# Neighbouring array groups for the state space products, and norms summed as their tiles are made

## The chip, the cores and the metric

One core of a Trainium2 chip runs the whole program. Its engines are TensorE (matrix products), VectorE, ScalarE, GpSimd and SyncE (which issues loads); they run side by side and wait for each other by semaphores. The metric is the device time of one execution in microseconds, the median of several.

## What is computed

The input is x of 512 tokens and 1024 features, a context of 256 tokens and a condition vector c. Two blocks follow each other. The first has a modulated norm, a two-way linear recurrence (LRU) beside a chunk-wise mixer, a second modulated norm with a convolutional feed-forward part, and a final norm:

```
rms(x, g)  = x * rsqrt(mean(x*x) + eps) * g
mod(x, g, shift, scale) = rms(x, g) * (1 + scale) + shift
m = silu(c) @ w_mod + b_mod                       # six rows: shift, scale, gate, twice
x = x + m[2] * mixer(mod(x, g1, m[0], m[1]) @ w_in)
x = x + m[5] * conv_ffn(mod(x, g2, m[3], m[4]))
h = rms(x, g_final)
```

The second block norms h again (mix_g) and adds two branches: S5, a complex diagonal state space, and an attention of 8 heads with a forget gate and with normed queries and keys. A third norm feeds a layer that picks 16 of 16384 experts per head and token:

```
xr, xi = u @ Br, u @ Bi                           # 32 groups of 16 inputs, 64 states
s_t    = lambda * s_(t-1) + x_t                   # complex
y      = sr @ Cr - si @ Ci + d * u
h = h + 0.25-scaled sum of glu(gelu(y)) and attention, through w_out
h = h + peer(rms(h, ffn_g))
```

## The kernel before

Everything lies with features on the 128 partitions and tokens along the row: a tensor of 1024 features is 8 tiles (k or d) of 128x512. The large products split both operands into a high and a low half (`split_w` L114 for weights: ScalarE copies the high half `whi`, VectorE subtracts for `wlo`; `split_to` L144 for activations) and need three products a tile (`mm3`, L121 to L123); `proj` makes one block of 128 output features from 8 tiles, 24 products.

A norm sums over features, so over partitions and tiles. `colsum` (L150) multiplies each squared tile by a block of ones, four tiles on the four groups of 32 output columns; `tok_mean` (L160) copies the result and turns the sums of 128 tokens into a column with a second small product, `c32` carrying the 1/1024; `rstd_of` (L166) takes root and reciprocal, and `bcast_tok` (L175, L176) spreads the result over all partitions as `pr` with four diagonal matrices `dg`. `scaled_split` (L181 to L186) multiplies a tile with `pr` and the gain, and splits it.

At the start SyncE loads the parameters, x, the context (`ct`) and the four modulation chunks of w_mod that this norm needs (chunks 0 and 1 are the shift's halves, 2 and 3 the scale's; two buffers `wm`). `mod_a` (L208) multiplies a chunk with the condition on four column groups, `mod_b` (L217 to L221) turns the result into columns of `modx` and `modc`. Then a loop over k (L278 on) scales, shifts and splits x and context tiles, and `lru_in` multiplies them with w_rx, two blocks a head.

The stages of the first block follow: LRU to 215 us, mixer with w_out to 637 us, the second norm with modulation chunks 10 and 11 (L208, ahead of it in the code), feed-forward to 1027 us, where `ffn_down` adds into x1, the final norm and the mixer norm one after the other to 1046 us. From 1060 to 1450 us an order written out by hand interleaves S5 and attention: for each pair of heads `a_proj`, `a_sums` (sums of squares of query and key, each on its own column group, L1032), `a_norm2` (spreads the reciprocal roots over partitions, L1044, and splits), `a_scores`, `a_trans`, `a_pv`, and between them 17 calls of `s5_step`. A step s of S5 stands for two groups, 32 inputs and 128 states: `s5_x` multiplies 32 rows of u with B's real and imaginary parts (L973, L974), VectorE rotates and scans them (L978 to L987), and in the next step `s5_y` (L1001) multiplies the four results with C into 32 partitions of `py`, four steps filling one `py`:

```
nc.tensor.matmul(pxr, BT[0][rows, q], uT[rows, q], start=True, stop=True)
nc.tensor.matmul(pxi, BT[1][rows, q], uT[rows, q], start=True, stop=True)
...
nc.tensor.matmul(py[32 * i:32 * i + 32], CD[c][:, s], x, start=n == 0, stop=n == 3)
...
nc.tensor.matmul(pb, selq[j], rs, start=True, stop=True)
```

Here `rows` are partitions 32i to 32i+32 with i = s mod 4, so neighbouring steps use neighbouring groups of 32 rows (B) and of 32 columns (C). w_glu and w2_out follow to 1567 us, then the third norm, transposes of x3, the queries, the selection (1582 to 1730 us) and the two expert stages with their gathers, which no part of the change touches. A scheduler orders each engine's instructions from the written order and the data, so a piece of code can move against its neighbours.

## Time and profile before

| what | value |
|---|---|
| time of three executions | 2935.10, 2935.18, 2942.08 us; median 2935.18 |
| profiled execution: time / span | 2937.33 / 2935.5 us |
| TensorE busy, products | 2846.1 us (97%) |
| TensorE's weight loads, beside them | 2293.1 us (78%) |
| VectorE, ScalarE, GpSimd busy | 1963.8, 1159.5, 404.2 us |
| mean granted clock of TensorE | 0.984 of full speed |
| instructions | 37882 |

PE is TensorE, PEld its weight loads, DVE VectorE, ACT ScalarE, POOL GpSimd, SP SyncE. A busy TensorE is not one at its peak: its products overlap in a pipeline, their ends are modelled, and a product alone is listed as longer than the distance to the next. A product in plain 32-bit is two records. The granted clock is a share of 2.4 GHz, so 0.5 is 1.2 GHz. An arrow names what ended an engine's wait. Idle time of an engine that nobody waits for costs nothing, so the shares are read stage by stage.

### The profile page before, as it was taken

To read this page: it belongs to the slowest core of one execution; us is meant where nothing else is said; L and a number is where in the kernel's file an instruction comes from. 1 tells how busy PE (TensorE), PEld (TensorE's weight loads), DVE (VectorE), ACT (ScalarE), POOL (GpSimd) and SP (SyncE) were. 2 spreads that over 40 slices of the span, in tenths; PEclk is the share of its full clock that TensorE was granted. 3 is DMA by queue.
4 is the path that set the end of the run, shared out by engine and by line. 5 is a ranking of instruction groups with operands and counts; after the bars stand their busy time and mean duration, and the time that the engine had idled before them with its cause. 6 is when DMAs were issued, how large, how long until landed. Compare 5 with 4: busy or idle time off the path is not lost.

```text
span 2935.5 us, 37882 instructions
## 1 busy us (share of the span) xinstructions
PE 2846.1 (97%) x14431; PEld 2293.1 (78%) x14431; DVE 1963.8 (67%) x3556; ACT 1159.5 (39%) x1599; POOL 404.2 (14%) x437
## 2 busy tenths in 40 slices
PE   8999999999999999999999989999989999999999
PEld 5778888867888866665787879898989977777776
DVE  6686894339767575777455999999875444444444
ACT  4666523223323333334433334555543333333332
POOL 0000000000000000000000034555433112222221
PEclk9999999999999999999999999999999999999999
DMA  6333363332333322222223258898997588888884
GB/s 253 111 128 96 102 195 118 102 124 93 98 96 93 103 103 72 74 72 63 94 93 115 84 172 309 301 330 315 329 353 269 195 294 295 309 304 318 315 309 161
DMA packets 167622, 540.16 MB, mean 184 GB/s; under 512 B 16912, under 2 KB 42128, under 8 KB 163984
## 3 DMA queue, kind: packets, MB, share of 16 engines
q1 hardware_dynamic: 128272, 391.94, 39.6%
q0 software_dynamic: 36864, 134.23, 12.4%
q10 hardware_dynamic: 2304, 11.57, 1.0%
q8 instruction: 113, 1.85, 0.3%
q14 instruction: 69, 0.57, 0.1%
HBM read 479.48 MB, written 58.20 MB: 183 GB/s over the span
## 4 chain that ended last, share of the span: by engine, by line
PE 80%; DVE 9%; issue 5%; ACT 2%; POOL 2%; DMA 1%; POOLq 0%; DVEq 0%; ACTq 0%
PE acc L1628 19%; PE pmm L121 15%; PE pmm L123 15%; PE pmm L122 15%; PE accg L1505 2%; PE pmm L1001 2%; DVE wlo L114 2%; POOL rows L1459 2%; DVE rows L1470 1%; PE pm L208 1%; PE pa L150 1%; PE pg L121 1%; PE pg L122 1%; PE pg L123 1%; PE pmm L973 1%
## 5 line engine op out<-in xcount | busy, mean ns | idle before, releaser
L113 ACT ACTIVATE whi<-raw 128x1024 fp32r<-128x1024 f32 (+2 forms) x502 | 518.1, 1033 | 910.6 <-PE pmm L122 741.7
L114 DVE TENSOR_TENSOR wlo<-raw,whi 128x1024 fp32r<-128x1024 f32 (+2 forms) x502 | 607.7, 1211 | 298.1 <-ACT whi L113 293.4
L123 PE MATMUL pmm<-nph,wlo 128*128 128x384 f32 (+1 forms) x1152 | 398.4, 346 | 18.5 <-DVE wlo L114 18.4
L121 PE MATMUL pmm<-nph,whi 128*128 128x384 f32 (+1 forms) x1152 | 405.1, 352 | 0.3 <-ACT whi L113 0.3
L122 PE MATMUL pmm<-npl,whi 128*128 128x384 f32 (+1 forms) x1152 | 396.5, 344 | 0.0
L144 DVE TENSOR_TENSOR wtl<-w,wth 128x384 fp32r<-128x384 f32 x128 | 71.3, 558 | 292.7 <-ACT wth L143 284.9
L1628 PE MATMUL acc<-whi,wth 128*128 128x512 f32 x768 | 245.0, 400 | 0.0
L1628 PE MATMUL acc<-wlo,wth 128*128 128x512 f32 x768 | 241.5, 396 | 0.0
L1628 PE MATMUL acc<-whi,wtl 128*128 128x512 f32 x768 | 241.5, 395 | 0.0
L123 PEld LDWEIGHTS pmm<-nph,wlo 128*128 128x128 f32 x1152 | 219.5, 191 | 27.9 <-DVE wlo L114 22.7
L121 PEld LDWEIGHTS pmm<-nph,whi 128*128 128x128 f32 x1152 | 220.2, 191 | 5.1 <-ACT whi L113 0.6
L122 PEld LDWEIGHTS pmm<-npl,whi 128*128 128x128 f32 x1152 | 220.0, 191 | 4.5
L143 ACT ACTIVATE wth<-w 128x384 fp32r<-128x384 f32 x128 | 67.1, 525 | 395.7 <-PE acc L1628 382.3
L1459 POOL DMA_INDIRECT rows<-in_peer_v_rows_dram,idxT x128 | 126.5, 988 | 503.5 <-PE accg L1505 400.5
L1470 DVE SCALAR_TENSOR_TENSOR rows<-rows,hN 128x1024 f32<-128x1024 f32 x128 | 155.0, 1217 | 50.3 <-DMA rows<-in_peer_u_rows_dram,idx 49.3
L1628 PEld LDWEIGHTS acc<-whi,wth 128*128 128x128 f32 x768 | 141.8, 188 | 58.6 <-ACT whi L113 26.8
L1459 POOL DMA_INDIRECT rows<-in_peer_u_rows_dram,idx x128 | 165.6, 1294 | 48.7 <-POOL rows L1458 26.4
L1628 PEld LDWEIGHTS acc<-wlo,wth 128*128 128x128 f32 x768 | 144.4, 188 | 34.9
L1628 PEld LDWEIGHTS acc<-whi,wtl 128*128 128x128 f32 x768 | 144.4, 188 | 34.8
L123 PE MATMUL pmm<-h2h,wlo 128*128 128x512 f32 x352 | 138.0, 394 | 2.8 <-DVE wlo L114 2.8
L121 PE MATMUL pmm<-h2h,whi 128*128 128x512 f32 x352 | 138.8, 396 | 1.7 <-ACT h2h L185 1.6
L122 PE MATMUL pmm<-h2l,whi 128*128 128x512 f32 x352 | 138.2, 394 | 0.1
(503 smaller groups left out, 5797.2 us busy)
## 6 DMA issues: line engine op xcount, KB each, us to landing
raw<-in_peer_u_dram SPq DMA_DIRECT2D x128, 512.0 KB
raw<-in_peer_v_rows_dram SPq DMA_DIRECT2D x128, 512.0 KB
GD<-G SPq DMA_DIRECT2D x12, 2048.0 KB
Gg<-GD SPq DMA_DIRECT2D x64, 384.0 KB
raw<-in_w_up_dram SPq DMA_DIRECT2D x44, 512.0 KB
AD<-act SPq DMA_DIRECT2D x48, 384.0 KB
act<-AD SPq DMA_DIRECT2D x48, 384.0 KB
raw<-in_w_mod_dram SPq DMA_DIRECT2D x32, 512.0 KB
```

What stands on the lines that cost most here:

```text
L113: nc.scalar.activation(hi[:, :n], raw[:, :n], AF.Copy)
L114: (eng or nc.vector).tensor_tensor(out=lo[:, :n], in0=raw[:, :n], in1=hi[:, :n].bitcast(F32), op=OP.subtract)
L121: nc.tensor.matmul(ps, wh, ah, start=first, stop=False)
L122: nc.tensor.matmul(ps, wh, al, start=False, stop=False)
L123: nc.tensor.matmul(ps, wl, ah, start=False, stop=last)
L143: nc.scalar.activation(hi, src, AF.Copy)
L144: nc.vector.tensor_tensor(out=lo, in0=src, in1=hi.bitcast(F32), op=OP.subtract)
L1001: nc.tensor.matmul(py[32 * i:32 * i + 32], CD[c][:, s], x, start=n == 0, stop=n == 3)
L1459: nc.gpsimd.indirect_dma_start(out=r, out_offset=None, in_=I[tab], in_offset=bass.IndirectOffsetOnAxis(ap=at, axis=0))
L1470: nc.vector.scalar_tensor_tensor(r, r, 1.0, hN, op0=OP.mult, op1=OP.mult, accum_out=dot[:, n:n + 1])
L1505: nc.tensor.matmul(acc[q][32 * g:32 * g + 32], w[:, g, 31 - c:63 - c], ready[g][:, q * 512:(q + 1) * 512], start=c == 0, stop=c == 31)
L1628: nc.tensor.matmul(acc[t][q], a[:, c], bb[:, q * 512:(q + 1) * 512], start=f, stop=l)
```

## The change

1. Start: loads come in the order chunk 2, chunk 0, two w_rx blocks, chunk 3, chunk 1. The squares of x are summed tile by tile on VectorE, those of the context on GpSimd, which also scales the context. The first half of the tiles is split after chunks 2 and 0, and the first two w_rx blocks are multiplied tile by tile as these come.
2. Norms: `SumSq` replaces `colsum` and `tok_mean`; each tile's square is added to one accumulator (GpSimd, or VectorE for the last), and one small product per 128 tokens gives the mean. It runs inside the loops of w_out, w_down and w2_out. After the second norm two w_up blocks advance tile by tile (`two`), and chunk 11 comes behind them. The final and the mixer norm take both sums at once and normalise by the product of their roots; two u blocks advance tile by tile. At the third norm one of four sets of transposes goes ahead.
3. S5 and attention: `s5_y` interleaves the products of step s with those of s-1; `s5_in` makes B's real part of the next step right behind the imaginary part of this one; `a_norm2` issues its four broadcasts together, each over its own 32 rows; three buffers for w1 and w2; one more call of `s5_step`.

The core of the diff:

```diff
+    class SumSq:
+        def add(self, src, eng=None, scale=1.0):
+            if self.k == 0:
+                nc.scalar.activation(self.acc, src, AF.Square, scale=scale)
+            else:
+                s = self.pool.tile([128, self.n], F32, name=self.sqtag, tag=self.sqtag, bufs=self.bufs)
+                nc.scalar.activation(s, src, AF.Square, scale=scale)
+                (eng or nc.vector).tensor_tensor(out=self.acc, in0=self.acc, in1=s, op=OP.add)
+            self.k += 1
+        def mean(self, pb):
+            for t in range(self.n // 128):
+                nc.tensor.matmul(pb[:, 2 * t:2 * t + 2], self.acc[:, t * 128:(t + 1) * 128], cD, start=True, stop=True)
+            return pb[:, 0:2 * (self.n // 128):2]
+    def sqrt_table():
+        nc.scalar.activation(junk, epsb, AF.Sqrt)
...
+    for ch in (2, 0, 3, 1):
+        wm[ch] = wk.tile([128, 8, 512], F32, name="wm", tag="wm", bufs=2)
...
+        if ch == 0:
+            rraw = [load_raw(I["w_rx"][n].rearrange("p k c -> p (k c)"), 1024) for n in range(2)]
...
+    for k in range(KT):
+        sc.add(ct[:, k], nc.gpsimd)
+    s_.append(mod_a(psp, wk, 0, whole=wm[0]))
+    rxw = [split_w(r, 1024) for r in rraw]
...
+    for k in range(KT):
+        nc.gpsimd.tensor_tensor(out=ct[:, k], in0=ct[:, k], in1=prcs, op=OP.mult)
...
+    h_tiles(0)
+    rx_mm(0, 2)
+    s_ = [mod_a(psp, wk, ch, whole=wm[ch], wide=ps2) for ch in (3, 1)]
+    rx_mm(2, 3)
+    for x, ch in zip(s_, (3, 1)):
+        mod_b(psp, x, ch, wide=ps2)
+    h_tiles(4)
+    rx_mm(3, KT)
...
         nc.vector.scalar_tensor_tensor(x1[:, d], pp, m2h[:, d:d + 1], x1[:, d], op0=OP.mult, op1=OP.add)
+        s2.add(x1[:, d], nc.gpsimd if d < KT - 1 else nc.vector)
...
+    r1 = rstd_of(const, s2.mean(psm()), T, "r1")
...
-    ms = [mod_a(ps, n2p, 10), mod_a(ps, n2p, 11)]
-    r1 = rstd_of(n2p, tok_mean(n2p, ps, sq_tiles(n2p, x1), T, "n2"), T, "r1")
-    mod_b(ps, ms[0], 10)
-    mod_b(ps, ms[1], 11)
+    ms = mod_a(ps, n2p, 10)
     pr = bcast_tok(n2p, ps, r1, T)
+    pg01 = [psm(), psm()]
     for k in range(KT):
         scaled_split(n2p, pr, A2[:, k:k + 1], x1[:, k], h2h[:, k], h2l[:, k], T, bias=modx[:, 24 + k:25 + k])
+        two(k, pg01, "w_up", (0, 1), h2h, h2l)
+    mod_b(ps, ms, 10)
+    mod_b(ps, mod_a(ps, n2p, 11), 11)
...
+        if k0 + kg == 22:
+            sa.add(x1[:, d], nc.gpsimd if d < KT - 1 else nc.vector)
+            sb.add(x1[:, d], scale=gf[:, d:d + 1])
...
+    for k in range(KT):
+        scaled_split(np_, pr12, gfm[:, k:k + 1], x1[:, k], hbh[:, k], hbl[:, k], T)
+        two(k, pu01, "w2_u", (0, 1), hbh, hbl)
...
+        px = S5["x", s, c] = psm()
+        nc.tensor.matmul(px, BT[c][rows, q], uT[rows, q], start=True, stop=True)
...
+        if s == 0:
+            s5_in(0, 0)
+        s5_in(s, 1)
+        if s < 15:
+            s5_in(s + 1, 0)
...
-        for n, (c, x) in enumerate(S5.pop(("s", s))):
-            nc.tensor.matmul(py[32 * i:32 * i + 32], CD[c][:, s], x, start=n == 0, stop=n == 3)
+        for n in range(2):
+            for u, j in ((s, n), (s - 1, 2 + n)):
+                if 0 <= u < 16:
+                    q, i = divmod(u, 4)
+                    if i == 0 and j == 0:
+                        S5["py", q] = psm()
+                    nc.tensor.matmul(S5["py", q][32 * i:32 * i + 32], CD[(0, 2, 1, 1)[j]][:, u], S5["s", u][j],
+                                     start=j == 0, stop=j == 3)
...
+        pbs = {j: psm() for j in (0, 2, 1, 3)}
+        for j, pb in pbs.items():
+            nc.tensor.matmul(pb, selq[32 * j:32 * j + 32], rs[32 * j:32 * j + 32], start=True, stop=True)
         for j in (0, 2, 1, 3):
-            pb = psm()
-            nc.tensor.matmul(pb, selq[j], rs, start=True, stop=True)
+            pb = pbs.pop(j)
...
+    s3 = SumSq(gp, T, "s3")
...
+    rows_of_x3(NTD)
+    pr = bcast_tok(n3, ps, r3, T)
```

SyncE's queue at the start of the program, before (`par` the parameters, `xt` x, `ct` the context, `wm` the chunks 0 to 3 in turn, `raw` weight blocks):

```order
L82 DMA par_66<-in_par_dram 128x489
L236 DMA xt_104<-in_x_dram 128x2048 x2
L238 DMA ct_107<-in_ctx_dram 128x2048
L243 DMA wm_109<-in_w_mod_dram 128x2048 x2
L243 DMA wm_112<-in_w_mod_dram 128x2048 x2
L243 DMA wm_115<-in_w_mod_dram 128x2048 x2
L243 DMA wm_118<-in_w_mod_dram 128x2048 x2
L107 DMA raw_407<-in_w_rx_dram 128x1024
```

and with the change, where the four `wm` are chunks 2, 0, 3, 1:

```order
L82 DMA par_66<-in_par_dram 128x489
L245 DMA xt_105<-in_x_dram 128x2048 x2
L247 DMA ct_108<-in_ctx_dram 128x2048
L253 DMA wm_110<-in_w_mod_dram 128x2048 x2
L253 DMA wm_113<-in_w_mod_dram 128x2048 x2
L108 DMA raw_116<-in_w_rx_dram 128x1024
L108 DMA raw_118<-in_w_rx_dram 128x1024
L253 DMA wm_120<-in_w_mod_dram 128x2048 x2
L253 DMA wm_123<-in_w_mod_dram 128x2048 x2
```

The two w_rx blocks now stand ahead of the last two chunks.

TensorE around the second norm, before (`pm` modulation, `pb` the mean, `pt` its columns, `pr` the spread reciprocal root, `h2h` the split result):

```order
L208 MATMUL pm_5143<-raw_5156,cz_84 32x512 x2
L160 MATMUL pb_5189<-c32_74,ssum_5187 128x2 x4
L217 MATMUL pt_5197<-sel2_78,ms_5141 128x2 x4
L217 MATMUL pt_5203<-sel2_78,ms_5160 128x2 x4
L176 MATMUL pr_5210<-dg_5209,ones_72 128x128 x4
L121 MATMUL pmm_5272<-h2h_5122,whi_5275 128x512
```

and with the change, from the last product of w_out (`mh`) on:

```order
L124 MATMUL pmm_5094<-mh_4546,wlo_5087 128x512
L166 MATMUL pmm_5136<-cD_74,u_4844 128x2 x4
L217 MATMUL pm_5165<-raw_5166,cz_85 32x512 x2
L217 MATMUL pm_5165<-raw_5170,cz_85 32x512 x2
L217 MATMUL pm_5165<-raw_5174,cz_85 32x512 x2
L217 MATMUL pm_5165<-raw_5178,cz_85 32x512 x2
L185 MATMUL pr_5185<-dg_5184,ones_72 128x128 x4
L122 MATMUL pmm_5194<-h2h_5163,whi_5121 128x512
L122 MATMUL pmm_5195<-h2h_5163,whi_5128 128x512
L226 MATMUL pt_5276<-sel2_79,ms_5182 128x2 x4
```

The mean (`cD`) now follows w_out at once, and two w_up blocks (`whi_5121`, `whi_5128`) start ahead of the columns of chunk 10.

TensorE at one step of S5 in attention, before (`sr`, `p2`, `w2`, `w1` are the step's four results, the numbers tell instances apart):

```order
L1001 MATMUL pmm_9022<-sr_8875,CD0_5111 32x512
L1001 MATMUL pmm_9022<-p2_8887,CD2_5113 32x512
L1001 MATMUL pmm_9022<-w2_8878,CD1_5112 32x512
L1001 MATMUL pmm_9022<-w1_8877,CD1_5112 32x512
L973 MATMUL pmm_9027<-uT_7978,BT0_5109 128x512
L974 MATMUL pmm_9028<-uT_7978,BT1_5110 128x512
```

and the same place with the change:

```order
L1082 MATMUL pmm_9008<-sr_9018,CD0_5152 32x512
L1082 MATMUL pmm_9008<-w2_8864,CD1_5153 32x512
L1082 MATMUL pmm_9008<-p2_9030,CD2_5154 32x512
L1082 MATMUL pmm_9008<-w1_8863,CD1_5153 32x512
L1042 MATMUL pmm_9109<-uT_8030,BT1_5151 128x512
L1042 MATMUL pmm_9111<-uT_8030,BT0_5150 128x512
```

`w2` and `w1` now come from the step before, between `sr` and `p2` of this one, and the real part of B (`BT0`) behind the imaginary one belongs to the next step.

## Rows read from the trace of the kernel before

**Rows 1.** The page's chain that ended last, shares of the span by engine.

```profile
PE 80%; DVE 9%; issue 5%; ACT 2%; POOL 2%; DMA 1%; POOLq 0%; DVEq 0%; ACTq 0%
```

**Rows 2.** Busy us by engine (instructions), granted clock and DMA share, five windows.

```profile
core 0: us, PE busy (x) PEld busy (x) DVE busy (x) ACT busy (x) POOL busy (x), PEclk, DMA share, GB/s
0.00:20.00 20.00, 10.66 (x52) 4.84 (x52) 7.16 (x46) 11.44 (x25) 0.43 (x5) 1.00 0.92 373
41.00:60.40 19.40, 19.15 (x96) 16.23 (x96) 16.30 (x33) 9.34 (x19) 0.35 (x6) 0.91 0.25 82
640.00:660.00 20.00, 15.32 (x70) 8.75 (x71) 6.75 (x14) 9.14 (x13) 0.00 (x0) 0.72 0.70 237
1089.00:1095.80 6.80, 6.80 (x20) 4.37 (x20) 5.75 (x10) 0.00 (x0) 0.00 (x0) 0.50 0.01 2
1221.70:1317.80 96.10, 96.10 (x410) 58.96 (x409) 69.87 (x103) 34.25 (x64) 0.00 (x0) 0.96 0.22 72
```

**Rows 3.** TensorE in w_out: start us, us, engine, line, operation, tiles, shapes.

```profile
631.73 0.39 PE L122 MATMUL pmm<-ml,whi 128*128 128x512 f32 x1
636.71 0.39 PE L123 MATMUL pmm<-mh,wlo 128*128 128x512 f32 x1
```

**Rows 4.** Timeline of VectorE, first and last instruction of the input tiles.

```profile
39.61 0.55 DVE L278 TENSOR_SCALAR nt<-xt,A,modx 128x512 f32<-128x512 f32 x1
58.76 0.42 DVE L144 TENSOR_TENSOR hcl<-nt,hch 128x256 fp32r<-128x256 f32 x1
```

**Rows 5.** GpSimd and VectorE at 1743 us; the page's weight subtractions.

```profile
1743.09 5.85 POOL L1374 TENSOR_TENSOR eq<-eq,idf 128x1024 f32<-128x1024 f32 x2 [0.68 <-DVE eq L1372]
1744.20 2.48 DVE L1363 TENSOR_TENSOR fb<-fpos,fs 128x128 f32<-128x128 f32 x1
1746.60 3.42 DVE L114 TENSOR_TENSOR wlo<-raw,whi 128x1024 fp32r<-128x1024 f32 x1
...
L114 DVE TENSOR_TENSOR wlo<-raw,whi 128x1024 fp32r<-128x1024 f32 (+2 forms) x502 | 607.7, 1211 | 298.1 <-ACT whi L113 293.4
```

**Rows 6.** Readers of h2h, 636.9 to 700: ns min/median/max, first, last start.

```profile
L121 PE MATMUL pmm<-h2h,whi x52: 389/389/796, 657.2 to 699.6; 128*128 128x512 f32 x52
```

**Rows 7.** TensorE by line, same stretch: busy us, mean ns, idle before.

```profile
L208 PE MATMUL pm<-raw,cz 128*32 128x512 f32 x32 | 8.5, 712 | 3.3 <-DMA raw<-in_w_mod_dram 3.3
```

**Rows 8.** Timeline of VectorE, last x1 tile and the second norm's reciprocal.

```profile
637.14 0.75 DVE L676 SCALAR_TENSOR_TENSOR x<-pmm,m2h,x 128x512 f32<-128x512 f32 x1 [4.69 <-PE pmm L123]
653.01 0.17 DVE L166 RECIPROCAL r<-r 128x4 f32<-128x4 f32 x1
```

**Rows 9.** Instructions that read hbh, 1027.3 to 1080 us.

```profile
L121 PE MATMUL pmm<-hbh,whi x46: 387/389/796, 1045.0 to 1079.8; 128*128 128x512 f32 x46
```

**Rows 10.** TensorE: B's products, sums in two column groups, broadcasts, C's products.

```profile
1085.45 1.12 PE L973 MATMUL pmm<-uT,BT 32*128 32x512 f32 x2
1086.42 1.02 PE L974 MATMUL pmm<-uT,BT 32*128 32x512 f32 x2
...
1090.30 1.92 PE L1032 MATMUL pmm<-qs,ones 128*32 128x512 f32 x4
...
1134.37 3.59 PE L1044 MATMUL pmm<-rs,selq 128*128 128x512 f32 x8
1137.89 1.04 PE L1001 MATMUL pmm<-sr,CD 128*32 128x512 f32 x2
...
1141.44 0.91 PE L121 MATMUL pmm<-qh 128*128 128x512 f32 x4
```

**Rows 11.** Timeline of VectorE: the split of the key of the first pair.

```profile
1138.98 0.68 DVE L144 TENSOR_TENSOR ql<-qf,qh 128x512 fp32r<-128x512 f32 x1
```

**Rows 12.** All waits of TensorE, 1060 to 1450 us: total, times, longest.

```profile
PE pmm L121 <- ACT ph L143: 1.1, 2, 0.8
```

**Rows 13.** Timeline of TensorE's weight loads among C's products.

```profile
1138.35 0.11 PEld L1001 LDWEIGHTS pmm<-p,CD 128*32 128x32 f32 x1 [0.32 <-issue]
```

**Rows 14.** Instructions that read nph, 1567 to 1620 us.

```profile
L121 PE MATMUL pmm<-nph,whi x48: 387/389/477, 1582.3 to 1619.0; 128*128 128x512 f32 x48
```

## What I expect of the change

> **What bounds the kernel now.** I read the page first. TensorE carries 80% of the chain that ended last, VectorE 9% [rows 1]. So what TensorE does one after the other, and its idle time at the seams between stages, is what can be won; a saving on another engine counts only where TensorE waits for it. I then cut the span into windows [rows 2]. In the attention cycle shown TensorE is busy all of its 96.10 us and VectorE 69.87 of them; the cycles beside it read alike; at the first products (41.00 to 60.40) VectorE is busy 16.30 of 19.40 us and sets the pace; at the second norm (640 to 660) TensorE is busy 15.32 of 20 us, at 0.72 of its clock. Last I read the places that the change touches, instruction by instruction. Nothing after 1600 us is touched; the top-k, the gathers and the two expert stages follow from the third norm's result, so what arrives earlier there ends earlier by as much.
>
> One unit is needed throughout. In w_out 22 products of 128x512 in split precision start within 631.73 to 636.71 us [rows 3]: 0.226 us for one, 5.4 us for a projection of 24.
>
> **Start: -9 us.** Before, scaling, shift and splitting of the inputs start at 39.61 us, when all four modulation chunks are there, and VectorE ends the eighth tile at 59.2 (58.76 + 0.42) [rows 4]. That is 2.2 us a tile once the weight subtractions are out of the way (58.76 and the tile before it, 56.58). The change loads scale chunk 2 and shift chunk 0 first, the two w_rx blocks next, and splits tiles 0 to 3 as soon as those two chunks are multiplied. Loads run at 373 GB/s in the first 20 us [rows 2]; parameters, x, context, two chunks (4 MB), the two blocks (1 MB) and the last two chunks (4 MB) are some 12.3 MB, so chunk 0 lands near 20 us and chunk 1 near 33. Multiplied and transposed, the first half of scale and shift is there near 24.5, and tiles 0 to 3 with the two subtractions of w_rx (4 x 2.2 + 2.4) are done near 36; the second half is there at about 39.5, when everything was there before. Four tiles of 2.2 us and one weight subtraction remain: VectorE ends near 49.5, against 59.2. I take 9 of these 9.7 us, for the following reason.
>
> The context's seven sums and eight scalings go to GpSimd. The trace shows what that does to VectorE: while two GpSimd products of 128x1024 ran (5.85 us), a VectorE product of 128x128 took 2.48 us and a weight subtraction 3.42 us [rows 5], where the page gives a subtraction 1211 ns on average. So the two block each other. Scaled by size, a GpSimd operation of 128x256 is an estimated 5.85 / 2 / 4 = 0.73 us, and the eight scalings, which fall beside tiles 0 to 3, can cost VectorE up to 5.9 us. Some 3.5 us of that lie in its wait for chunk 1, from 36 to 39.5. Bounds of this term: 3 us (all of it exposed and the loads late) to 13 (chunk 1 early, DMA unhindered).
>
> **Second norm: -13 us.** From the last w_out product to 700 us, 155 products start (52, 52 and 51 in three lines, one shown, the first at 657.2) [rows 6]. They are worth 155 x 0.226 = 35.0 of 63.1 us; 28 us are norm, modulation and waiting. In that time lie modulation chunks 10 and 11 (8.5 us of records) [rows 7], with the column sums among them. The change squares each x1 tile when it is made (ScalarE, the sum on GpSimd, the last on VectorE), and one set of small matmuls gives the mean. From the last x1 tile, which starts at 637.14 and takes 0.75 [rows 8], follow square and sum (about 1.3), mean (1.1) and root (0.4): the reciprocal ends near 640.8, where it starts at 653.01 now. (The change's dummy root, which would load ScalarE's table early, stands at the program's start in the compiled order, so the load stays before this root; it can run while sum and mean do.) From it to the first product it takes 4.2 us now [rows 6, 8], one weight subtraction of 1.2 among them that the change has behind it: first product near 644. Two w_up blocks then advance tile by tile, six products (1.36 us) against two VectorE operations (1.40). Chunk 11, which was ahead of the norm, moves into this stretch: an estimated 2 to 3 us, and a wait for a weight subtraction as today some 2 more. Non-product time falls from 28 to about 14; I take 13, bounds 10 and 17. The sums on GpSimd block a w_out subtraction by 1.5 us each; in w_out each has 5.4 us, and that hides it.
>
> **Final and mixer norm: -8 us.** The same in the next seam: 137 products (46, 46, 45) by 1080 us, the first at 1045.0 [rows 9], worth 31.0 of 52.7 us, so 21.7 are other work: two norms in a row, the second over the first's result. The change sums both squares while w_down still runs, takes both roots from the two means and normalises with their product; first product near 1036. VectorE then paces the two u blocks, and part of the 9 us is given back: 8, bounds 6 and 10.
>
> **State space products and head norms: -37 us.** Before, a step's four products with C take from 1137.89 to 1141.44 us, 3.55 us, and its two with B 1.94 (twice the 0.97 from 1085.45 to 1086.42), each waiting for the one ahead; a head norm's four broadcasts take 3.52 (1134.37 to 1137.89) [rows 10]. Over 16 steps and 4 calls that is 56.8, 31.0 and 14.1 us. The change interleaves step s with s-1, so that neighbours write different column groups; lets B's imaginary part of s be followed by the real part of s+1, which lie in other row groups; and contracts each broadcast over its own 32 rows. For column groups the trace has the answer: at 1090.30 two sums in neighbouring groups, four records, take 1.92 us in a stretch with the clock at 0.50 [rows 2, 10], so 0.96 at full clock, against 1.78 for four of C's in series. C then costs 17 x 1.92 = 32.6, a saving of 24.2. For row groups no row exists: between nothing and the same overlap I take the same overlap, since column groups are the nearest row. B's products then save 14 and the broadcasts 10 (four groups at once: eight records in about 0.96). Together 48.
>
> Against this stands a new wait. Today the scores start at 1141.44, though query and key are split at 1139.66 [rows 10, 11]; the shorter broadcasts and C products bring TensorE there at 1134.37 + 0.96 + 1.92 = 1137.3, so it now waits for VectorE some 2.5 us, 4 times: 10 us; and I add 1 us to its one wait of today in this stage, 1.1 us for the split of the probabilities [rows 12], since less work stands ahead of it. That leaves 37. Bounds: 10 (row groups in series, and C's gain halved) and 48. VectorE stays under the limit: 70 us in a cycle that shrinks from 96 to some 87.
>
> On weight loads a row and a rule differ. C's loads take 0.11 us each, and start between the products [rows 13]; at 1090.30 the four overlapping records, loads included, fit into 1.92 us. The Trainium skill, "TensorE: Matmul & The Clock Gate", Part 3, says that a weight load overlaps running matmuls only when the row groups differ; C's neighbours share all rows, so by that rule eight loads a step, 17 x 8 x 0.11 = 15 us, would come back and the whole sum be -56. The row speaks against it here.
>
> **Third norm: -3.5 us.** From w2_out to 1620 us, 144 products (48 in each line, the first at 1582.3) [rows 14]: 32.5 of 53 us. Sixteen column-sum records wait for squares; the change has the sums ready and puts a quarter of the 32 transposes before the norm. But splitting eight tiles on VectorE stays ahead of the query products, so only some of it is won: 1 to 5.
>
> **Sum.** -9 - 13 - 8 - 37 - 3.5 = -70.5. The profiled execution took 2937.33 us (span 2935.5), 2.2 above the median of the runs, 2935.18. So 2866.8, and 2864.7 against the median; I say 2866.
>
> **The rivals.**
> (a) Row groups don't overlap. No row speaks for or against. B's and the broadcasts' 24 us stay away, and with them about 8 of the 11 us of new waits: -70.5 + 16, about 2883.
> (b) Column neighbours pay their weight loads, or VectorE's chain through the steps (products, two scans, four products) becomes what TensorE waits for. For: VectorE is busy 73% of a cycle, and the cycle shrinks. Against: the waits lie at few places. The loads' 15 us or, the same size, 2 us at each of 8 heads: 2882.
> (c) It does more: new waits find other work, chunk 11 fits in. All upper bounds, 13 + 17 + 10 + 48 + 5 = 93: 2844.
> (d) Slower: the clock. Stretches at 0.50 exist in this stage (1089.0 to 1095.8, 6.8 us) [rows 2] right behind small products at full clock, and one costs half its length, 3.4 us. If shorter, packed products and new waits drop the clock throughout the stage, the gain is gone from 21 such stretches on (70.5 / 3.4), that is 143 us of the 390; if the whole stage ran so, its 350 us of products would nearly double and the time be about 3190. Against: there are only a few of them today, behind other kinds of work too.
> (e) It doesn't do what it says: the compiler's order undoes the interleaving, or the loads come in the old order. The order of instructions printed above has the new order on TensorE and on the load queue, so it would have to lie in the seams; if none of them moved, 2900.
>
> **How the numbers follow.** My forecast 0.55; (a) 0.17; (b) 0.13; (c) 0.07; (d) 0.03; (e) 0.05. A measurement of this kernel tells 0.3%, 9 us, from no change. Forecast, (a), (b) and (c) are faster by more, 0.92, and so is (e) where only the seams stay, 0.02: 0.94. The rest of (e) is the same, 0.03; (d) is slower, 0.03. The forecast's own range by its bounds is 2852 to 2882. For 8 in 10, I take in (a), (b) with the poor ends of the start and the seams, and most of (c): 2846 to 2900.
>
> **What would show it.** Right: records with C in two column groups starting nearly together, the stage's 3.55 us at 1.9; B's pair and the broadcasts the same; TensorE waiting for the split of query or key before the scores; first products near 644 and 1036, the first stage ending near 50. The step on row groups is wrong if B's neighbours start 0.43 us apart. The forecast is wrong if VectorE is over 90% busy in the cycles, or the granted clock in them under 0.9, or if the start is no earlier because subtractions beside GpSimd take over 2 us.

## The result, and the profile after

The changed kernel takes 2902.21 us (median of four runs, 2901.61 to 2903.16), the kernel before, measured beside it, 2938.63. The ratio is 0.9879, with an interval of 0.9863 to 0.9895. It is faster, by half of what was forecast: 2866 was said, and the range ended at 2900.

The page of the changed kernel, busy time and chain by engine (answers to [rows 1]):

```profile
span 2900.9 us, 37769 instructions
...
PE 2793.5 (96%) x14335; PEld 2274.1 (78%) x14335; DVE 1976.4 (68%) x3569; ACT 1157.0 (40%) x1597; POOL 448.0 (15%) x470
...
PE 80%; DVE 9%; issue 4%; POOL 2%; ACT 2%; DMA 2%; DVEq 0%; POOLq 0%; SPq 0%; ACTq 0%
```

TensorE has 52.6 us less to do (2846.1 before), the span is 34.6 shorter: 18 us of the work saved came back as waiting. A ledger of TensorE's marks tells where: the start of the last or first product of a stage, in the profiled execution of each kernel (2937.33 and 2902.67 us).

| mark on TensorE | before | after | this stretch | forecast |
|---|---|---|---|---|
| last product with x of the first w_rx head | 59.93 | 62.41 | +2.5 | -9 |
| last w_out | 636.71 | 640.91 | +1.7 | 0 |
| last w_down (second norm and feed-forward) | 1027.15 | 1029.05 | -2.3 | -13 |
| first B (final and mixer norm) | 1062.94 | 1058.35 | -6.5 | -8 |
| first w_glu (S5 and attention) | 1451.44 | 1415.47 | -31.4 | -37 |
| last w2_out | 1566.88 | 1532.50 | +1.6 | 0 |
| first key product (third norm) | 1594.23 | 1554.05 | -5.8 | -3.5 |
| last product of the last expert stage | 2930.51 | 2895.93 | +5.6 | 0 |
| sum | | | -34.6 | -70.5 |

**The start.** TensorE's timeline of the changed kernel: start us, us, engine, line, operation, tiles, shapes, and in brackets the idle time before and what ended it.

```profile
24.61 0.68 PE L185 MATMUL pr<-dg,ones 128*128 128x128 f32 x4 [2.92 <-DVE dg L184]
25.13 1.19 PE L226 MATMUL pt<-sel,ms 128*128 128x2 f32 x8
26.25 1.93 PE L217 MATMUL pm<-wm,cz 128*32 128x512 f32 x8
...
48.20 1.06 PE L217 MATMUL pg<-wm,cz 128*32 128x512 f32 x8
```

VectorE's, in the same kernel:

```profile
19.19 4.87 DVE L265 TENSOR_TENSOR xt<-xt,pr 128x512 f32<-128x512 f32 x8 [1.32 <-PE pr L185]
...
30.80 0.16 DVE L228 TENSOR_TENSOR modx<-pt,par 128x4 f32<-128x4 f32 x1 [3.46 <-PE pt L226]
31.00 0.64 DVE L291 TENSOR_SCALAR nt<-xt,A,modx 128x512 f32<-128x512 f32 x1
...
51.13 0.16 DVE L228 TENSOR_TENSOR modx<-pg,par 128x4 f32<-128x4 f32 x1 [4.36 <-PE pg L226]
...
60.41 0.42 DVE L145 TENSOR_TENSOR hcl<-nt,hch 128x256 fp32r<-128x256 f32 x1
```

And SyncE's load queue and GpSimd, two answers of the same timeline:

```profile
20.21 8.83 SPq L253 DMA_DIRECT2D wm<-in_w_mod_dram  x4
...
25.85 5.51 POOL L275 TENSOR_TENSOR ct<-ct,prcs 128x256 f32<-128x256 f32 x8 [4.82 <-DMA wm<-in_w_mod_dram]
```

The first half of scale and shift is there at 30.96 and the second at 51.29; forecast were 24.5 and 39.5. VectorE ends its last tile at 60.8, where 49.5 was forecast. The reader can follow the queue upwards. VectorE scales x for 4.87 us before it makes the context's `dg`; TensorE waits 2.92 us for that at 24.61, because the spread of the context's norm (`pr`) stands ahead of chunk 2's columns (25.13) and of chunk 0's last products (26.25). Those products hold a `wm` buffer, so the load queue's last four issues take until 29.04. Even so the last of these loads, issued at 28.6, is in 7.1 us later, near 35.7, where the forecast had chunk 1 near 33 (answer for this issue alone; its last number is the time to landing in us):

```profile
wm<-in_w_mod_dram SPq DMA_DIRECT2D x1, 1024.0 KB, 7.1
```

But chunk 1's products stand in TensorE's order behind chunk 3's and behind the w_rx products of the first tiles, and the last of them run at 48.20. TensorE does not wait in that time, it works through its queue (window, columns as in [rows 2]):

```profile
32.30:49.30 17.00, 16.66 (x88) 10.37 (x88) 8.73 (x20) 4.56 (x10) 0.00 (x0) 0.89 0.47 193
```

GpSimd's scalings were over at 31.36, when the splits had just begun.

**The second norm.** TensorE's timeline from the last w_out product (640.91) on:

```profile
643.66 1.87 PE L166 MATMUL pmm<-cD,u 128*128 128x2 f32 x8 [2.36 <-DVE u L160]
645.46 3.64 PE L217 MATMUL pm<-raw,cz 128*32 128x512 f32 x16
649.03 1.77 PE L185 MATMUL pr<-dg,ones 128*128 128x128 f32 x8
652.39 0.73 PE L122 MATMUL pmm<-h2h,whi 128*128 128x512 f32 x2 [1.60 <-ACT h2h L194]
```

The window of the mean and chunk 10 (columns as in [rows 2]):

```profile
643.60:649.00 5.40, 5.34 (x24) 2.37 (x24) 1.06 (x6) 0.77 (x2) 0.00 (x0) 0.50 0.14 12
```

And the readers of the three norms' results, in stretches as long as those of [rows 6], [rows 9] and [rows 14] (63.1, 52.7 and 53 us; three answers):

```profile
L122 PE MATMUL pmm<-h2h,whi x59: 388/389/628, 652.4 to 704.2; 128*128 128x512 f32 x59
...
L122 PE MATMUL pmm<-hbh,whi x48: 389/389/795, 1040.6 to 1076.5; 128*128 128x512 f32 x48
...
L122 PE MATMUL pmm<-nph,whi x56: 389/389/478, 1542.9 to 1585.2; 128*128 128x512 f32 x56
```

With their two sister lines these are 175 products where 155 stood, 144 for 137, and 168 for 144. So the second norm's seam is worth 20 x 0.226 = 4.5 us; the forecast wanted 13. The first product follows w_out by 11.5 us (20.5 before, 7 forecast), and the stretch before it ran at half clock; of these 9 us, half is lost again behind the first product. In the second stretch the count says less than the ledger, because more products of S5 fall into it than before (ten records of B where there were four); there the first product follows w_down by 11.5 us instead of 17.8.

**State space products.** TensorE's timeline: the four broadcasts, a whole step of C, B's pair, and a step where `py` changes.

```profile
1123.40 1.14 PE L1129 MATMUL pmm<-rs,selq 32*128 32x512 f32 x8
...
1144.28 1.13 PE L1042 MATMUL pmm<-uT,BT 32*128 32x512 f32 x4
...
1153.41 0.62 PE L1117 MATMUL pmm<-qs,ones 128*32 128x512 f32 x2
1153.42 0.62 PE L1082 MATMUL pmm<-sr,CD 128*32 128x512 f32 x1
1153.43 0.62 PE L1082 MATMUL pmm<-w,CD 128*32 128x512 f32 x1
...
1154.74 0.59 PE L1082 MATMUL pmm<-w,CD 128*32 128x512 f32 x1
1155.26 1.13 PE L1042 MATMUL pmm<-uT,BT 32*128 32x512 f32 x4
...
1162.77 1.90 PE L1082 MATMUL pmm<-w,CD 128*32 128x512 f32 x4
...
1176.48 1.05 PE L1082 MATMUL pmm<-sr,CD 128*32 128x512 f32 x2
1177.37 1.02 PE L1082 MATMUL pmm<-p,CD 128*32 128x512 f32 x2
```

Both kinds of groups overlap. The broadcasts' eight records take 1.07 us to the next start, 3.52 before [rows 10]; B's four 1.06 against 1.94; C's eight 1.84 (1153.42 to 1155.26) against 3.55. In the step shown four records of a head norm's sums (L1117, the first two at 1153.41) run in the other two column groups in the same time, so all four groups overlap; a step without them, at 1188.28, takes 1.84 us too. At 1162.77 and 1176.48 the partners are apart: a new `py` begins there, and the products stand alone.

TensorE's four longest waits in the stage (total us, times, longest; L1056 is the S5 arithmetic on VectorE, `qh` and `ql` the split of queries and keys, `ph` that of the probabilities):

```profile
PE pmm L1082 <- DVE p L1056: 2.3, 3, 1.3
PE pmm L122 <- ACT qh L144: 1.9, 2, 1.5
PE pmm L122 <- ACT ph L144: 1.6, 2, 0.8
PE pmm L123 <- DVE ql L145: 1.1, 2, 0.6
```

All eleven lines add up to 11.5 us, where before there was one line of 1.1 [rows 12].

### The profile page after: what moved, and what is told of

It reads as the page before. It is cut to its first block, busy times and chain, and to the rows that moved or that the text cites. A ratio compares the mean times of both kernels' runs of the same rounds, so it can differ in the third digit from the quotient of the medians.

```text
span 2900.9 us, 37769 instructions
## 1 busy us (share of the span) xinstructions
PE 2793.5 (96%) x14335; PEld 2274.1 (78%) x14335; DVE 1976.4 (68%) x3569; ACT 1157.0 (40%) x1597; POOL 448.0 (15%) x470
## 3 DMA queue, kind: packets, MB, share of 16 engines
q0 software_dynamic: 36864, 134.23, 12.6%
q8 instruction: 112, 1.84, 0.3%
## 4 chain that ended last, share of the span: by engine, by line
PE 80%; DVE 9%; issue 4%; POOL 2%; ACT 2%; DMA 2%; DVEq 0%; POOLq 0%; SPq 0%; ACTq 0%
PE acc L1721 19%; PE pmm L122 16%; PE pmm L123 16%; PE pmm L124 16%; PE accg L1598 2%; DVE wlo L115 2%; POOL rows L1552 2%; DMA rows<-in_peer_u_rows_dram,idx 1%; PE pm L217 1%; PE pmm L1082 1%; PE pg L122 1%; PE pg L123 1%; PE pg L124 1%; DVE rows L1563 1%; ACT whi L114 1%
## 5 line engine op out<-in xcount | busy, mean ns | idle before, releaser
L124 PEld LDWEIGHTS pmm<-nph,wlo 128*128 128x128 f32 x1152 | 219.7, 191 | 31.3 <-DVE wlo L115 26.0
```

What stands on the lines that cost most here:

```text
L124: nc.tensor.matmul(ps, wl, ah, start=False, stop=last)
```

## The experiments

Each is compared with the kernel before, as the result was.

**Part 3 alone**, in the kernel before:

```diff
-        for n, (c, x) in enumerate(S5.pop(("s", s))):
-            nc.tensor.matmul(py[32 * i:32 * i + 32], CD[c][:, s], x, start=n == 0, stop=n == 3)
+        for n in range(2):
+            for u, j in ((s, n), (s - 1, 2 + n)):
...
-            nc.tensor.matmul(pb, selq[j], rs, start=True, stop=True)
+            nc.tensor.matmul(pb, selq[32 * j:32 * j + 32], rs[32 * j:32 * j + 32], start=True, stop=True)
```

> The kernel before with the third part alone (interleaved C products, B's real part beside the next step's row group, the four broadcasts over 32 rows each). If the trace of the change is read rightly, the attention stage gains 31 us and nothing else moves: about 2937 - 31 = 2906. If the forecast's term holds and other parts of the change spoiled it, -37: 2900. If the gain depended on the norms arriving earlier, less than 25: over 2912.

2907.71 us, 0.9894 (0.9875 to 0.9913): 30.7 us less than 2938.39. The part alone gives what the ledger says of its stage, 31.4, and nothing of it is lost later. It also shows how far the start varies without an edit: this kernel starts with the code of before, and its first head ended at 63.48, not 59.93.

**Part 1 alone**, in the kernel before (and the constants it needs):

```diff
+    cD = const.tile([128, 2], F32, name="cD")
+    junk = const.tile([128, 1], F32, name="junk")
...
-    for ch in range(4):
+    for ch in (2, 0, 3, 1):
```

> The kernel before with the new start alone (order of loads, running sums, half of the tiles split early). Account from the trace of the change: the second half of the shifts comes at 51 us instead of 39 because its chunk is loaded and multiplied behind the context's chain, so the first w_rx head ends 2.5 us later: about 2939.5, slower by 1 to 4. Forecast's term: -9, 2928.

2924.26 us, 0.9946 (0.9931 to 0.9961). The head ended at 63.10, so the start gains nothing; yet the whole was faster, most of it in the last expert stage, which the edit doesn't touch. The new constants move every weight buffer in memory, and this was the first sign of what the next run tests. The kernel before with an unused constant, further down, runs w_pr and the last stage at the same paces as this one (0.2267 and 0.2275 us a product) and takes 2922.2 us: the moved buffers account for all of this run's gain.

**One 16-byte constant moved to another pool**, in the changed kernel, so that the buffers behind the constants shift (in the layout each of the small constants takes 32 bytes):

```diff
-    r2, r12 = (const.tile([128, 4], F32, name=n) for n in ("f2", "f12"))
+    r2 = np_.tile([128, 4], F32, name="f2")
+    r12 = const.tile([128, 4], F32, name="f12")
```

> The change with one 32-byte constant moved to another pool, so that weights and left-hand tiles lie 128 bytes instead of 160 bytes further than before; no instruction is added or taken away. Theory: the products of w_pr, w_pg, w_down, w_glu and w2_out, whose two operands moved against each other by 160 bytes, go 2% slower by that alone; then the pitch of 0.234 us goes back to 0.229 and the time falls by 4 to 5 us, 2897 to 2898. Rival: the pitch comes from what other engines do beside the products; then nothing changes, 2902.

2893.21 us, 0.9843 (0.9825 to 0.986): 9 us less for no change in the work. The theory was right that addresses count, and wrong in which way: the stages meant to gain stayed slow, the last expert stage gained 9.6 us.

**All three constants moved**, so that operand and weight buffer agree modulo 256 bytes in the program's memory layout:

```diff
-    gfm = const.tile([128, 8], F32, name="gfm")
+    gfm = np_.tile([128, 8], F32, name="gfm")
...
-    r2, r12 = (const.tile([128, 4], F32, name=n) for n in ("f2", "f12"))
+    r2, r12 = (np_.tile([128, 4], F32, name=n) for n in ("f2", "f12"))
```

> The change with three 32-byte constants moved to another pool, so that weights lie 64 bytes further than before, and their addresses equal those of the left-hand tiles and of the last stage's wth modulo 512. Theory of addresses: all products of these stages go at 0.227 us (0.234 in the change), the last stage's at 0.2275 (0.2334): -9 and -13.5 us, 2880. Rival, that the 9 us of the shift by 128 were another thing that the moved constant did: 2893.

2876.8 us, 0.9791 (0.9778 to 0.9805): 25.4 us less than the change. TensorE's readers of the mixer's `ygh`, a stage that the change leaves alone, in the kernel before, the changed one, the one with one constant moved and the one with three (four answers; ns min/median/max, first and last start):

```profile
L121 PE MATMUL pmm<-ygh,whi x64: 394/394/397, 549.4 to 592.7; 128*128 128x512 f32 x64
```

```profile
L122 PE MATMUL pmm<-ygh,whi x64: 392/397/400, 552.6 to 596.9; 128*128 128x512 f32 x64
```

```profile
L122 PE MATMUL pmm<-ygh,whi x64: 394/394/394, 554.1 to 598.2; 128*128 128x512 f32 x64
```

```profile
L122 PE MATMUL pmm<-ygh,whi x64: 389/389/390, 553.3 to 596.1; 128*128 128x512 f32 x64
```

The same 192 products take 43.3, 44.3, 44.1 and 42.8 us. In the last expert stage, of before, the change and three constants moved:

```profile
L1628 PE MATMUL acc<-wlo,wth x768: 393/396/398, 2327.9 to 2930.0; 128*128 128x512 f32 x192
```

```profile
L1721 PE MATMUL acc<-wlo,wth x768: 392/394/399, 2293.3 to 2895.5; 128*128 128x512 f32 x192
```

```profile
L1721 PE MATMUL acc<-wlo,wth x768: 389/389/398, 2280.7 to 2869.6; 128*128 128x512 f32 x192
```

602.1, 602.2 and 588.9 us: of the 25.9 us between the two profiled executions 13.3 are won here, 12.6 before the stage begins. Not all of the 12.6 is the addresses': in this run the second norm stayed at full clock, and its first product came 3.1 us sooner after w_out than in the change.

**The kernel before with an unused constant**, 64 bytes, and in a second version 320 (one buffer of the first norm's squares is left out to make room); nothing else is changed:

```diff
+    spare = const.tile([128, 16], F32, name="spare")
+    nc.vector.memset(spare, 0.0)
...
-        s = wk.tile([128, n], F32, name="sq", tag="sq", bufs=4)
+        s = wk.tile([128, n], F32, name="sq", tag="sq", bufs=3)
```

> The kernel before with nothing but an unused constant of 64 bytes ahead of the weight buffers (and three square buffers instead of four in the first norm, to make room for it). Theory of addresses: weights and left-hand tiles then agree modulo 512, as in the change's version with 64 bytes; w_pr, w_pg, w_down, w_glu, w2_out at 0.227 instead of 0.229 us and the last stage at 0.2275 instead of 0.2333: 2938 - 17 = 2921. If the pitch came with the change's code, nothing moves: 2938.

> As before64 with 320 bytes: the two addresses then differ by 256 bytes modulo 512. If what counts repeats every 256 bytes or less, the same as before64, about 2921; if it repeats only every 512, the pitch stays above 0.227 in those stages, and the time is that of the kernel before or more, 2935 to 2950.

2922.2 us, 0.9945 (0.993 to 0.996), and 2922.16, with the same ratio and interval. The same line of the last expert stage, with 64 bytes:

```profile
L1630 PE MATMUL acc<-wlo,wth x768: 387/389/398, 2327.5 to 2916.4; 128*128 128x512 f32 x192
```

588.9 us where the kernel before has 602.1. So addresses alone are worth 15 us in the kernel before too, and 256 bytes more make no difference: the effect repeats with 256 bytes or a part of that.

**Chunks 10 and 11 out of the second norm**: the products that were in the seam run in the feed-forward loop.

```diff
-    ms = mod_a(ps, n2p, 10)
...
-    mod_b(ps, ms, 10)
-    get_w("w_up", 22)
-    get_w("w_up", 2)
-    mod_b(ps, mod_a(ps, n2p, 11), 11)
...
+        if j in (1, 3):
+            mod_b(ps, mod_a(ps, fp, 10 + j // 2, mbufs=1), 10 + j // 2)
```

> The change with the second norm's result spread over the partitions at once, and modulation chunks 10 and 11 multiplied inside the feed-forward stage (behind blocks 1 and 3) instead of ahead of it. Theory: chunk 10 stands ahead of the spread root at half clock and chunk 11 waits for its load, together 8 us of the seam, of which about 4 come back as their own product time inside the stage or stay as low clock: 2896 to 2898. Rival: the seam is bound by VectorE's splitting and the low clock alone, 2902.

2903.37 us, 0.988 (0.9861 to 0.9899): no difference. The first product followed w_out by 8.4 us instead of 11.5, but from w_out to the last w_down only 1.3 us of these 3.1 were left: most of what the chunks had cost in the seam they cost in the loop. The edit also takes out the early fetch of two weight blocks (`get_w`), which isn't told apart.

**Chunks first** (with the three constants moved, as all that follow): the columns of chunks 2 and 0 ahead of the context's norm, those of 3 and 1 ahead of the w_rx products.

```diff
+    s_.append(mod_a(psp, wk, 0, whole=wm[0]))
+    for x, ch in zip(s_, (2, 0)):
+        mod_b(psp, x, ch)
...
-    s_.append(mod_a(psp, wk, 0, whole=wm[0]))
...
-    for x, ch in zip(s_, (2, 0)):
-        mod_b(psp, x, ch)
...
-    rx_mm(0, 2)
     s_ = [mod_a(psp, wk, ch, whole=wm[ch], wide=ps2) for ch in (3, 1)]
-    rx_mm(2, 3)
     for x, ch in zip(s_, (3, 1)):
         mod_b(psp, x, ch, wide=ps2)
+    rx_mm(0, 3)
```

> As align64, with the start's code reordered: modulation chunks 2 and 0 turned into columns ahead of the context's root, chunks 3 and 1 ahead of the w_rx products. Theory, that the start is late because chunk products and columns stand behind the context's chain and behind w_rx products: 6 to 10 us below align64, 2870 to 2874. Rival, that the late loading of chunk 1 (its buffer comes free late) sets it: 0 to 3 below align64, since buffers and loads stay.

2869.21 us, 0.9765 (0.9747 to 0.9783). Scale and shift are there at 24.86 and 43.89 us, where the change had 30.96 and 51.29, and the head ends at 54.24 instead of 64.01 with the constants moved alone. Against the starts of the kernel before this is 5.7 us (59.93) or 9.2 us (63.48, in Part 3 alone) earlier. So most of the forecast's gain of the start was there to be had; the order of the queues withheld it. The load queue hangs on the same order: with chunk 0's products earlier, its last four issues are out by 23.76 instead of 29.86, which the rival named in the expectation had taken as fixed. Now the splits do meet GpSimd's scalings. GpSimd and then VectorE in this kernel, two answers:

```profile
30.47 6.66 POOL L277 TENSOR_TENSOR ct<-ct,prcs 128x256 f32<-128x256 f32 x8 [9.66 <-ACT prcs L275]
...
34.44 1.22 DVE L145 TENSOR_TENSOR hxl<-nt,hxh 128x512 fp32r<-128x512 f32 x1
...
38.11 0.69 DVE L145 TENSOR_TENSOR hxl<-nt,hxh 128x512 fp32r<-128x512 f32 x1 [0.38 <-ACT hxh L144]
```

The same subtraction takes 1.22 us beside GpSimd (until 37.13) and 0.69 after it. The Trainium skill, "SBUF — State Buffer", section "SBUF: two separate sides", says that one port pair is shared by the two and held for a whole instruction; these rows agree with it.

**The context's sums and scalings on VectorE**, in the changed order and in that of the run before:

```diff
-        sc.add(ct[:, k], nc.gpsimd)
+        sc.add(ct[:, k])
...
-        nc.gpsimd.tensor_tensor(out=ct[:, k], in0=ct[:, k], in1=prcs, op=OP.mult)
+        nc.vector.tensor_tensor(out=ct[:, k], in0=ct[:, k], in1=prcs, op=OP.mult)
```

The second version moves the scalings alone.

> As align64, with the context's sums and scalings on VectorE instead of GpSimd. If GpSimd blocking VectorE (forecast's reservation) made the start late, this is faster by 2 to 5 us. If it did not, the 15 operations of about 0.35 us on VectorE stand in its queue: the same or up to 4 us slower.

> As al_chunks_first, with the context's scalings on VectorE (its sums stay on GpSimd). In al_chunks_first VectorE's splits took 0.95 to 1.22 us instead of 0.41 to 0.68 while GpSimd scaled. If that blocking cost time, the first head of w_rx ends 1 to 3 us earlier (54.2 there); if VectorE's own 2.7 us for the scalings weigh as much, no change. The total within 3 us of 2869.

2873.35 us, 0.9774 (0.9757 to 0.9792), and 2868.03, 0.9762 (0.9746 to 0.9778). In the changed order the head ended 5.3 us earlier (58.70). That isn't the context's doing: its `dg` came no sooner (24.42 us, and 24.02 with the constants alone), but the last products of chunk 1 stand further ahead on TensorE (44.46 instead of 49.46), so the second half of scale and shift is there at 48.42 instead of 52.55. At the last w_down the trace is level with that of the constants alone: 3.1 us were lost at the second norm, which ran at half clock in it, and the rest up to the last w_down, and why isn't known. The medians differ by 3.5 us, with runs from 2866 to 2879. With the chunks first the head ended no earlier (55.92), and the time is the same. So the slower subtractions beside GpSimd, though real, decide nothing here.

**Ten products that nobody reads**, behind w_out, to keep TensorE busy up to the mean:

```diff
+    warm = psm()
+    for k in range(10):
+        nc.tensor.matmul(warm, mh[:, 0, 0:128], mh[:, k % 8], start=k == 0, stop=k == 9)
```

> As align64, with ten products more at the end of w_out whose result nobody reads, so that TensorE is busy while VectorE squares and sums the last tile. Theory, that the second norm's term failed by the half clock which follows TensorE's 2.4 us of idleness (mean 1.87 us, chunk 10 3.64, spread root 1.77 against 1.05, 1.92 and 1.1): 2 to 3.5 us faster than align64, the first product with h2h 2 to 3 us earlier. Rival, that the seam is set by VectorE and ScalarE alone: the same.

> As al_cf_dve with the ten unread products behind w_out. The idle 2.36 us ahead of the second norm's mean brought the half clock in the change and in al_ctx_dve, but not in align64. Theory: whether it falls there hangs on when the stage comes, and busy products keep it up: first product with h2h 8.3 us after w_out instead of 10 to 11.5, time 1 to 3 us under al_cf_dve, or the same where that ran at full clock too.

2875.11 us, 0.9784 (0.9768 to 0.9799), and 2867.31, 0.9756 (0.9741 to 0.9771). The clock stayed full, but it did so in the profiles of their two partners without the products as well, so what the products are worth isn't settled. The last is the fastest median of all, 34.9 us under the change and 70.1 under the kernel before; from 2868.03 and 2869.21 its difference is within their spread.

What the clock costs at this seam, two kernels tell with the same idle time before the mean. With the constants moved, TensorE's window and timeline:

```profile
642.80:645.60 2.80, 2.77 (x24) 1.39 (x24) 1.05 (x5) 0.74 (x2) 0.00 (x0) 1.00 0.00 0
...
642.83 1.05 PE L166 MATMUL pmm<-cD,u 128*128 128x2 f32 x8 [2.36 <-DVE u L160]
643.81 1.92 PE L217 MATMUL pm<-raw,cz 128*32 128x512 f32 x16
```

and with the context on VectorE besides:

```profile
637.00:642.00 5.00, 4.93 (x24) 1.99 (x24) 1.06 (x6) 0.78 (x2) 0.00 (x0) 0.55 0.08 13
...
637.07 1.49 PE L166 MATMUL pmm<-cD,u 128*128 128x2 f32 x8 [2.36 <-DVE u L160]
638.48 3.64 PE L217 MATMUL pm<-raw,cz 128*32 128x512 f32 x16
```

At 2.4 GHz the 24 records take 2.8 us, in the other run 5 us and, as in the change, most of it at 1.2 GHz; the first product follows w_out by 8.3 us in the one and by 11.4 in the other.

## Why the prediction was wrong

The direction was right and the largest term nearly so; the time missed the range's end by 2 us, because the gain was half of that forecast. The lower bounds of the five terms add up to 30 us (3, 10, 6, 10 and 1), so 2907 was still within them, though not within the range; two terms, the start and the second norm, ended below their own lower bounds. By its own steps:

**Start (-9, measured +2.5 in the one profile, nothing in the runs): wrong.** The failed step is "Multiplied and transposed, the first half of scale and shift is there near 24.5" and, from it, "the second half is there at about 39.5". Both took the loads for the limit, and the loads came nearly as said (chunk 1 near 35.7, for 33). What decided were the instructions that stand ahead in TensorE's order: the context's `pr`, waiting for VectorE's eight scalings, and then the w_rx products. The run with the chunks first moved only that order and took 9.8 us off the head and 7.6 off the median. The suspected cause, GpSimd's scalings, was over before the splits came.

**Second norm (-13, measured -4.5 in the seam and -2.3 to the last w_down): wrong in size.** The failed step is "first product near 644", 7 us after w_out. It was costed at full clock; the trace has the mean and chunk 10 at 0.50, which makes 11.4 out of 8.3 us by the two runs above. Sixteen records of chunk 10 also stand ahead of `pr` (3.64 us), a place that the printed order showed and the sum left out. "An estimated 2 to 3 us" for chunk 11 was 5.9 (668.0 to 673.9, with a wait of 1.87 for its load). Moving the chunks away won nothing, so most of their price is that of the work. The feed-forward part lost 2.4 us to the addresses (528 products of w_down at 0.2340 instead of 0.2294).

**Final and mixer norm (-8, measured -6.5): right.** The first product was at 1040.6, not near 1036, but w_down ended 1.9 us later than before: it followed w_down by 11.5 us, where 17.8 stood and 9 were forecast. These 6.3 us are nearly the whole gain; from the first product to the first B both kernels take about 18 (18.0 and 17.8).

**State space products (-37, measured -31.4; alone -30.7): right in how the products overlap, one size off, and the waits right in sum only.** B's, C's and the broadcasts' products cost 43.2 us less, not 48. B (31.3 to 17.8) and the broadcasts (14.1 to 4.3) came as said. C took 37.4, not the "17 x 1.92 = 32.6": three times in 16 steps a new `py` parts the partners, and each such step takes 1.90 + 1.91 instead of 1.84, and the two ends have no partner either (15 x 1.84 + 2 x 1.9 + 3 x 1.97 = 37.3). Whether another order would keep them together wasn't tried. The new waits were 10.4 us, for 11 forecast, but that the sum fits is in part luck: the wait for the split of queries and keys, costed at 10 us, is 3.0 (`qh` 1.9, `ql` 1.1), and waits for S5's arithmetic on VectorE (L1056), which the sum didn't have, are 4.3 (2.3 of them in the line shown). VectorE is busy 68.93 of 82.70 us in the cycle where it had 69.87 of 96.10 [rows 2], 83%, and the clock is full:

```profile
1204.80:1287.50 82.70, 80.83 (x409) 53.06 (x408) 68.93 (x103) 34.23 (x64) 0.00 (x0) 1.00 0.25 82
```

So rivals (a) and (d) fall, and of (b)'s 15 us the 4.3 of S5's arithmetic are all that is seen. (e) named 2900 for a change whose seams don't move; the time is near that, but by another way, since the norms' seams did move and the products gave less. The rule of the Trainium skill on weight loads ("TensorE: Matmul & The Clock Gate", Part 3) would have made eight loads a step visible; the trace has eight records, loads included, in 1.84 us, and neighbours starting 0.01 us apart while they share all rows. The measurement disagrees with the rule here, as [rows 13] let expect.

**Third norm (-3.5, measured -5.8): right in direction**, and 0.8 us over its upper bound of 5.

**What the prediction didn't have.** "Nothing after 1600 us is touched ... what arrives earlier there ends earlier by as much" failed, by 5.6 us. VectorE's waits for gathered rows, of before and of the change:

```profile
DVE rows L1470 <- DMA rows<-in_peer_u_rows_dram,idx: 49.3, 26, 5.6
```

```profile
DVE rows L1563 <- DMA rows<-in_peer_u_rows_dram,idx: 56.2, 28, 5.1
```

The stretch from the last key product to the end of this stage is 641.4 us before, 646.2 after. In the eight other kernels with the change's third norm it is 644.5 to 646.1, in the four other kernels that keep the old one 640.9, 642.1, 643.9 and 648.4. So the longer stretch may come with the change, but one profile of each doesn't show it, and why stays open. And the addresses: five small constants (32 bytes each, so the distance went from +64 to -96) slowed the mixer's, the feed-forward's and the second block's products by some 6 us in all, which no view of the kernel before could show.

Of the 36 us between forecast and result, the start and the stretch behind it hold 13, the second norm 11, S5 and attention 6, and the last stages 6; the rest cancels. That the aligned kernel with its chunks first then takes some 2869 us, near the 2866 forecast, is luck: its order won 7.6 us, near the start's term of 9, but most of the rest comes from the addresses, which the forecast didn't have.

## What to carry to other kernels

When loads or products are moved forward, follow each in-order queue upwards: here it was what stood ahead of the moved piece on the engine that consumes it that decided, not when the data landed. Price the short products in a seam at both clock levels, since the same code with the same pause before it ran at either. And when a change adds or removes even a few bytes of buffers, compare the pitch (start to start) of products that it doesn't touch, before an effect is put down to the code.

## What the hardware showed that was not expected

**A product's pace went with the addresses of its operands.** Start to start, a 128x512 split product took, on average within its blocks of 24, by how far the left-hand tile lies behind its weight buffer in the program's layout, modulo 256 bytes:

| distance | kernel | w_pr | w_glu | w_down |
|---|---|---|---|---|
| 0 | three constants moved | 0.2267 us | 0.2267 | 0.2267 |
| +64 | before | 0.2295 | 0.2294 | 0.2294 |
| -64 | one constant moved | 0.2333 | 0.2333 | 0.2334 |
| -96 | the change | 0.2341 | 0.2341 | 0.2340 |

In the last expert stage the weights are the left-hand operand, so a shift of the weight buffers counts with the opposite sign; by the distance of the left-hand operand behind the other it is 0.2275 at 0, 0.2291 at +64, 0.2333 at -64 and 0.2334 at +96. w_out, whose tile stands at 0 in every one, kept 0.2267 to 0.2269. That the addresses are the cause is shown by the runs with an unused constant; what in the chip makes it so is not. Nor do they settle the pace alone: w_out's mate in the second block, w2_out, has the distance +64 and the same addresses in the kernel before and in Part 3 alone, and from its second block on it ran at 0.229 us in the one and at 0.233 in the other:

```profile
L121 PE MATMUL pmm<-nh,whi x64: 392/392/505, 1522.9 to 1566.4; 128*128 128x512 f32 x64
```

```profile
L121 PE MATMUL pmm<-nh,whi x64: 394/397/502, 1492.0 to 1536.2; 128*128 128x512 f32 x64
```

**Row groups overlap nearly as fully as column groups**: B's pair in two row groups is 1.83 times as fast as one after the other, C's in two column groups 1.93 times, and the eight records of four broadcasts in four row groups, in 1.07 us, 3.3 times.

**The clock fell in some runs and not in others** after the same 2.36 us of idle time at the second norm, behind the same products. Which it will be, these runs don't tell.
